# Norm factors of five groups spread by DRAM instead of by TensorE, and a new order in a run of small matmuls

## The chip, the core and the metric

The kernel runs on one core of a Trainium2 chip. The metric is the device time of one execution in microseconds (us); a time is the median of several runs. The engines are named as in the profile: PE is TensorE's matmuls, PEld its weight loads, DVE is VectorE, ACT is ScalarE, POOL is GpSimd, SP is SyncE, whose queue issues most of the loads. Each engine works through its own list of instructions in order. DRAM is the chip's main memory, SBUF and PSUM are the two memories beside the engines.

## What is computed

One decoder layer on 256 tokens of width 1024. One wide projection feeds a state-space scan (32 heads in 8 groups) and a causal attention (16 heads, two for each group), gates merge the two, an output projection and a gated feed-forward part follow. The part that the change touches is the end of the scan, where each group of 256 channels is normed by itself:

```python
y = y * jax.nn.silu(z.astype(jnp.float32))
yg = y.reshape(b, s, SSD_N_GROUPS, SSD_D_INNER // SSD_N_GROUPS)
yg = yg * lax.rsqrt(jnp.mean(yg * yg, axis=-1, keepdims=True) + RMS_EPS)
y = yg.reshape(b, s, SSD_D_INNER) * norm_w.astype(jnp.float32)
```

So each group has one factor for each of the 256 tokens (the rsqrt), and all 256 channels of the group are multiplied by it and by their own norm weight.

## The kernel before

Activations lie with channels on the 128 partitions and tokens along the row; a group's 256 channels are two halves of 128 x 256. Weights come in units of 1 MB by SP's queue into three buffers (`raw`). Each unit is split in two halves, and each half into a high part by ACT (`hi`, L96) and a low part by DVE (`lo`, L104); there are four buffers for each, which is two units. PE multiplies high by high, high by low and low by high (L165 to L167, L196 to L198, L460 to L462, and later L175 and L179).

The input stage (18 to 317 us of the profiled execution) is a loop over the groups g = 0 to 7. A group has the units `u_bc`, `u_x`, `u_qk`, `u_z`, and a value unit `u_v` or two gate units; between them lie two runs of small matmuls:

- `small_1(g)`, after `u_x(g)`: the scan's output of group g-1 (`s_y`, tile py, L521), the attention scores of g-1 (`a_s`, tile s_ps, L550), the attention output of g-2 (`a_o`, tile po, L608), the norm factors of g-2 (`s_pb`, tile pb, L242).
- `small_2(g)`, after `u_z(g)` or in the middle of the gate units: products for the scan of g (`s_cb`, `s_mx`, `s_xt`), the sum of squares of g-1 (`s_st`, tile stat, L231), and ACT's part of turning the probabilities of g-1 (`a_t`, L588).

How the norm goes: `s_y` leaves the gated output in yg and its squares in the buffer of zt, under the name sqy (L527, L528). `s_st` lets PE sum the squares over the partitions, which leaves the tokens on the partitions, 128 x 2; DVE makes the rsqrt by three Newton steps in small instructions (`rms_rstd`, the last is L222) and leaves it in ry, 128 x 2. `s_pb`, one group later, brings the factors back along the row on every partition: two PE matmuls (`rms_bcast`, L242) write them to pb in PSUM, and DVE multiplies yg by the norm weight and by pb (L537, two instructions). `split_pair` then makes the high part (ACT, L204) and the low part (DVE, L205) of yn, which only the projection behind the loop reads (from 303 us on). yg and zt have two buffers each, so those of group g come free for group g+2.

Attention: `a_s` lets DVE take the maxima (L557), ACT the exponentials and the scaling (L561, L565), POOL copy the probabilities as 16-bit halves (L571, two copies a group), and SP issue two transposing DMAs (L573), which stand in the same queue as the weight loads. `u_qk` copies q and k to SBUF (ACT, L435), POOL issues two small DMAs that swap their rotated rows (L437, L438), DVE multiplies by the cosines (L441), and `turn_qk` adds the sine part (L448, L449). POOL also issues the load of the scan's sums spread over the partitions (acsB, L424) and, in even groups, two loads of gate biases (L728).

What sets the order: PE's list is the program order. The lists of DVE, ACT, POOL and SP are made by a planner that follows the dependences, the program order as priority, and marks such as `tc.issue_after(x)` (not ahead of x in the list of that engine). A tile waits for the last reader of the buffer that it takes.

Of the kernel before, what the change touches and what calls it, by code (L numbers as in the profile page):

```python
# [8 lines left out]
F32 = mybir.dt.float32  # L9
# [4 lines left out]
ALU = mybir.AluOpType  # L14
# [5 lines left out]
P = 128  # L20
# [3 lines left out]
NG = 8  # L24
# [7 lines left out]
C_NW, C_D = 24, 40  # L32
# [5 lines left out]
C_ID = 256  # L38

WARM = 9  # L40


def block_kernel(tc, xtok_d, head_d, par_d, nf_d, con_d, rope_d, win_d, wgate_d, bg_d, watt_d, wssd_d, wout_d, wup_d, wdn_d, out_d):
    nc = tc.nc
    st = ExitStack()
    pool = lambda name, bufs=1, **kw: st.enter_context(tc.tile_pool(name=name, bufs=bufs, **kw))
    with st:
# [3 lines left out]
        dram = pool("dram", space=DRAM)  # L51
# [29 lines left out]
        def col(c):  # L81
            return par[:, c : c + 1]
# [141 lines left out]
        def rms_stat(sqs, inv_n):  # L224

            ps = ps_s.tile([P, 2, T], F32, tag="acc", bufs=1, name="stat")
            jobs = [(sq, ones[:, 0:1]) for sq in sqs]
            with tc.manual_schedule(engines=PE_ONLY):
                for i, (sq, one) in enumerate(jobs):
                    for c in range(2):  # L230
                        nc.tensor.matmul(ps[:, 0, c : c + 1], sq[:, c * P : c * P + P], one,  # L231
                                         start=(i == 0 and c == 0), stop=(i == len(jobs) - 1 and c == 1))
            y = work.tile([P, 2], F32, tag="ry", bufs=2, name="ry")
            with tc.high_priority():
                rms_rstd(y, ps[:, 0, 0:2], inv_n)
            return y

        def rms_bcast(y):

            pb = ps_s.tile([P, 2, T], F32, tag="ss", bufs=2, name="pb")  # L240
            for c in range(2):
                nc.tensor.matmul(pb[:, 0, c * P : c * P + P], y[:, c : c + 1].to_broadcast([P, P]), ident,  # L242
                                 start=True, stop=True)
            return pb[:, 0, :]
# [181 lines left out]
        def u_qk(g):  # L426
            hv = next_unit()
            if g == 0:

                with tc.issue_after(split_half.lo.ins):  # L430
                    conv_silu(S[0]["xs"], S[0]["x_ps"], (0, 1))
            ps = mm_tile()
            mm_unit(ps, hv, hn)
            raw = atp.tile([P, 2, T], F32, tag="qkraw", bufs=1, name="qkraw")
            S[g]["qk_copy"] = nc.scalar.activation(raw, ps, AF.Copy)  # L435
            sw = swaps[g % 2]
            nc.gpsimd.dma_start(sw[48:80:2], raw[49:80:2])  # L437
            nc.gpsimd.dma_start(sw[49:80:2], raw[48:80:2])  # L438
            qk = S[g]["qk"] = atp.tile([P, 2, T], F32, tag="qk", bufs=2, name="qk")
            cosb = rope[:, 0:1, :].to_broadcast([P, 2, T])  # L440
            nc.vector.tensor_tensor(qk, raw, cosb, op=ALU.mult)  # L441

        def turn_qk(g):

# [83 lines left out]
            nc.vector.tensor_tensor(sqy[:, 0], sqy[:, 0], sqy[:, 1], op=ALU.add)  # L528

        def s_st(g):  # L530
            S[g]["ry"] = rms_stat([S[g]["sqy"][:, 0]], 1.0 / 256)

        def s_pb(g):
            rb = rms_bcast(S[g]["ry"])
            yg = S[g]["yg"]
            for m in range(2):
                nc.vector.scalar_tensor_tensor(yg[:, m], yg[:, m], col(C_NW + 2 * g + m), rb, op0=ALU.mult, op1=ALU.mult)  # L537
                p = new_pair("yn")
                split_pair(p, yg[:, m])
                yn[2 * g + m] = p  # L540
# [154 lines left out]
        def small_1(g):  # L695
            if 0 <= g - 1 < NG:
                s_y(g - 1)
                a_s(g - 1)
            if 0 <= g - 2:
                a_o(g - 2)  # L700
                if g < NG:
                    s_pb(g - 2)

        def small_2(g):
            if g < NG:
# [10 lines left out]
        for g in range(NG):  # L716
            if g:
                u_bc(g)
                if g == 1:
                    s_mx(0, split_half.last_hi)  # L720
                u_x(g)
                small_1(g)
                load_acs(g)
            u_qk(g)
            if g % 2 == 0:
                cols = slice(256 * g, 256 * g + 512)
                for c in range(2):
                    tc.keep_in_program_order(nc.gpsimd.dma_start(gates[:, c, cols], bg_d[cols].partition_broadcast(P)))  # L728
            if g == 0:
                u_z(g, dt_sums)  # L730
                dt_turn()
                turn_qk(g)
                gate = u_gate(0)
                next(gate)
                load_acs(0)
                next(gate)
                next(gate)
                small_2(g)
                next(gate)
            elif g == NG - 1:  # L740
                u_z(g)
                turn_qk(g)
                small_2(g)
                u_v(g)
            elif g % 2:
                if g > 1:
                    u_v(g)
                    turn_qk(g)
                u_z(g)
                if g == 1:  # L750
                    turn_qk(g)
                small_2(g)
            else:
                u_z(g)
                turn_qk(g)
                gate = u_gate(g // 2)
                next(gate)
                next(gate)
                small_2(g)
                next(gate)  # L760
                next(gate)
# [319 lines left out]
```

## Time and profile before

| | |
|---|---|
| Time, median of 3 runs | 590.02 us (589.52 to 590.57) |
| The profiled execution, its own time | 589.48 us |
| Its span, from the first to the last instruction | 587.7 us |
| Granted TensorE clock, mean | 0.997 |
| PE busy | 579.0 us, 99% of the span |
| DVE busy | 464.0 us, 79% |
| ACT busy | 384.2 us, 65% |
| POOL busy | 33.7 us, 6% |
| Mean DMA rate | 191 GB/s |

The share of busy time says little for PE, since matmuls overlap and their ends are modelled: the start times tell what a matmul costs. What counts for the others is whether PE ever waits for them. The profile was taken of one execution; it is 0.54 us below the median of the runs.

### The profile page before, as it was taken

Reading aid. Unit: us, or ns where it says so; the run is one execution under the profiler, and the core shown is the slowest. Engines: PE = TensorE matmul, PEld = TensorE weight load, DVE = VectorE, ACT = ScalarE, POOL = GpSimd, SP = SyncE. Lnnn points to the kernel's source line nnn. Section 1 sums busy time; section 2 is a strip of 40 time slices with the busy share of each in tenths; the row PEclk is TensorE's granted clock in tenths of the full one; section 3 lists DMA queues with packets and bytes.
Section 4 is the critical chain, followed back from the end, with each engine's and each line's share of the span. In section 5 each row is a group of like instructions: output and inputs, shape, how many; then the busy total and the mean of one; then the engine's idle time right before and its main releaser. Section 6 shows DMA issues by size and latency. Waiting matters only on the chain.

```text
span 587.7 us, 9931 instructions
## 1 busy us (share of the span) xinstructions
PE 579.0 (99%) x3784; PEld 519.8 (88%) x3784; DVE 464.0 (79%) x891; ACT 384.2 (65%) x673; POOL 33.7 (6%) x55
## 2 busy tenths in 40 slices
PE   8999999999999999999999999999999999999995
PEld 8999999899998999989988888889888888888884
DVE  3996989899798997998996555768888898884643
ACT  2855697967769677695794434466777767774432
POOL 0010020301002010020100000000000000000100
PEclk9999999999999999999999999999999999999998
DMA  8766644874729737297436756554456545464601
GB/s 307 267 216 221 251 134 150 248 285 108 241 79 250 285 100 253 74 282 252 111 136 235 244 202 198 170 204 146 172 187 215 197 166 210 151 219 143 235 41 73
DMA packets 29136, 112.50 MB, mean 191 GB/s; under 512 B 13456, under 2 KB 13712, under 8 KB 17440
## 3 DMA queue, kind: packets, MB, share of 16 engines
q1 hardware_dynamic: 26320, 103.17, 52.1%
q0 software_dynamic: 2336, 6.85, 4.1%
q10 hardware_dynamic: 432, 1.84, 0.8%
q8 instruction: 30, 0.49, 0.3%
q14 instruction: 18, 0.15, 0.1%
HBM read 107.49 MB, written 1.08 MB: 185 GB/s over the span
## 4 chain that ended last, share of the span: by engine, by line
PE 98%; DMA 1%; DVE 0%; issue 0%; ACT 0%; DVEq 0%; ACTq 0%
PE up L175 12%; PE mm L165 11%; PE mm L167 11%; PE mm L196 11%; PE mm L166 11%; PE mm L198 11%; PE mm L197 11%; PE up L179 7%; PE py L521 2%; PE mm L294 1%; PE s_ps L550 1%; PE po L608 1%; PE mm L460 1%; PE mm L462 1%; PE mm L461 1%; PE pb L242 1%
## 5 line engine op out<-in xcount | busy, mean ns | idle before, releaser
L104 DVE TENSOR_TENSOR lo<-raw,hi 128x1024 fp32r<-128x1024 f32 x183 | 226.0, 1243 | 64.7 <-ACT hi L96 63.2
L96 ACT ACTIVATE hi<-raw 128x1024 fp32r<-128x1024 f32 x183 | 191.4, 1056 | 116.0 <-PE mm L198 62.0
L165 PE MATMUL mm<-hn,hi 128*128 128x256 f32 x504 | 143.6, 285 | 0.0
L167 PE MATMUL mm<-hn,lo 128*128 128x256 f32 x504 | 142.6, 283 | 0.0
L166 PE MATMUL mm<-hn,hi 128*128 128x256 f32 x504 | 142.6, 283 | 0.0
L165 PEld LDWEIGHTS mm<-hn,hi 128*128 128x128 f32 x504 | 96.6, 192 | 0.5 <-ACT hi L96 0.3
L166 PEld LDWEIGHTS mm<-hn,hi 128*128 128x128 f32 x504 | 96.7, 192 | 0.2
L167 PEld LDWEIGHTS mm<-hn,lo 128*128 128x128 f32 x504 | 96.6, 192 | 0.2 <-DVE lo L104 0.2
L175 PE MATMUL up<-xw,hi 128*128 128x512 f32 x320 | 76.3, 391 | 0.0
L175 PEld LDWEIGHTS up<-xw,hi 128*128 128x128 f32 x320 | 58.8, 188 | 11.4
L393 DVE SCALAR_TENSOR_TENSOR cacc<-mm,par,cacc 128x255 f32<-128x255 f32 (+2 forms) x96 | 44.1, 475 | 2.8 <-ACT cacc L389 2.3
L179 PEld LDWEIGHTS up<-xw,lo 128*128 128x128 f32 x320 | 41.0, 191 | 1.6
L179 PE MATMUL up<-xw,lo 128*128 128x256 f32 x320 | 41.5, 283 | 0.0
L197 PE MATMUL mm<-lo,act 128*128 128x512 f32 (+1 forms) x92 | 35.0, 380 | 0.0
L196 PE MATMUL mm<-hi,act 128*128 128x512 f32 (+1 forms) x92 | 34.9, 380 | 0.0
L198 PE MATMUL mm<-hi,act 128*128 128x512 f32 (+1 forms) x92 | 34.9, 380 | 0.0
L898 DVE SCALAR_TENSOR_TENSOR facc<-ab,par,facc 128x255 f32<-128x255 f32 (+1 forms) x44 | 21.2, 483 | 11.4 <-ACT facc L896 10.6
L196 PE MATMUL mm<-hi,hn 128*128 128x512 f32 x64 | 25.5, 398 | 0.0
L196 PE MATMUL mm<-hi,yn 128*128 128x512 f32 x64 | 25.2, 394 | 0.0
L198 PE MATMUL mm<-hi,hn 128*128 128x512 f32 x64 | 25.0, 391 | 0.0
L197 PE MATMUL mm<-lo,hn 128*128 128x512 f32 x64 | 25.0, 390 | 0.0
L198 PE MATMUL mm<-hi,yn 128*128 128x512 f32 x64 | 24.9, 390 | 0.0
(210 smaller groups left out, 978.8 us busy)
## 6 DMA issues: line engine op xcount, KB each, us to landing
raw<-in_win_dram SPq DMA_DIRECT2D x34, 1024.0 KB, 5.3
raw<-in_wup_dram SPq DMA_DIRECT2D x22, 1024.0 KB, 4.7
raw<-in_wdn_dram SPq DMA_DIRECT2D x10, 1024.0 KB, 4.9
raw<-in_wgate_dram SPq DMA_DIRECT2D x8, 1024.0 KB, 5.4
raw<-in_wssd_dram SPq DMA_DIRECT2D x8, 1024.0 KB, 4.9
acsB<-acsT_d POOLq DMA_DIRECT2D x8, 512.0 KB, 6.0
raw<-in_watt_dram SPq DMA_DIRECT2D x4, 1024.0 KB, 5.2
raw<-in_wout_dram SPq DMA_DIRECT2D x4, 1024.0 KB, 5.2
```

The source lines that it names most:

```text
L96: split_half.hi = nc.scalar.activation(hi[:, :n], raw[:, k0 : k0 + n], AF.Copy)
L104: split_half.lo = nc.vector.tensor_tensor(lo[:, :n], raw[:, k0 : k0 + n], hi[:, :n].bitcast(F32), op=ALU.subtract)
L165: nc.tensor.matmul(ps[m], wh, xh, start=a, stop=False)
L166: nc.tensor.matmul(ps[m], wh, xl, start=False, stop=False)
L167: nc.tensor.matmul(ps[m], wl, xh, start=False, stop=z)
L175: nc.tensor.matmul(ps[:, m].rearrange("p a b -> p (a b)"), hi[:, kk, m * P : m * P + P], act[k].rearrange("p a b -> p (a b)"), start=(k == ...
L179: nc.tensor.matmul(ps[:, m, 1], lo[:, kk, m * P : m * P + P], act[k][:, 0, :], start=False, stop=(k == len(tiles) - 1))
L196: nc.tensor.matmul(o, xh, wh, start=(k == 0 if apart else k0 + k == 0), stop=False)
L197: nc.tensor.matmul(o, xh, wl, start=False, stop=False)
L198: nc.tensor.matmul(o, xl, wh, start=False, stop=(k0 + k == nk - 1))
L393: nc.vector.scalar_tensor_tensor(acc[:, s:], src[:, m, : T - s], w(m, 3 - s), acc[:, s:], op0=ALU.mult, op1=ALU.add)
L898: nc.vector.scalar_tensor_tensor(acc[:, s:], src[:, : T - s], w(2 - s), acc[:, s:], op0=ALU.mult, op1=ALU.add)
```

## The change

For the groups 1 to 5 the factors no longer go through PE. Behind the rsqrt, `s_st` has POOL write ry to a small tensor in DRAM (each partition writes its two values, a piece of 8 bytes, 128 pieces), and then read it back for all 128 partitions (1 KB each) into the second half of sqy, which nobody needs any more. The second DMA waits until the first has landed. There the tokens lie interleaved (token t of both token halves side by side), so DVE reads every second value. `s_pb` of these groups has no matmul; its two multiplications read the factors from SBUF and are held behind the cosine product of two groups later, and `s_pb` itself moves from `small_1(g+2)` to behind `u_qk(g+2)`. The groups 0, 6 and 7 keep the matmuls. In every `small_1` the attention output (`a_o`) now comes ahead of the scores (`a_s`): scan, attention output, scores.

```diff
+BY_DRAM = (1, 6)
...
-            nc.vector.tensor_tensor(qk, raw, cosb, op=ALU.mult)
+            S[g]["qk_cos"] = nc.vector.tensor_tensor(qk, raw, cosb, op=ALU.mult)
...
         def s_st(g):
-            S[g]["ry"] = rms_stat([S[g]["sqy"][:, 0]], 1.0 / 256)
+            sqy = S[g]["sqy"]
+            ry = S[g]["ry"] = rms_stat([sqy[:, 0]], 1.0 / 256)
+            if BY_DRAM[0] <= g < BY_DRAM[1]:
+                rd = dram.tile([P, 2], F32, tag="rd", bufs=2, name="rd")
+                nc.gpsimd.dma_start(rd, ry)
+                S[g]["rb"] = sqy[:, 1].rearrange("p (t c) -> p c t", c=2)
+                nc.gpsimd.dma_start(sqy[:, 1], rd.rearrange("p c -> (p c)").partition_broadcast(P))
 
         def s_pb(g):
-            rb = rms_bcast(S[g]["ry"])
+            by_dram = "rb" in S[g]
+            rb = S[g]["rb"] if by_dram else rms_bcast(S[g]["ry"])
             yg = S[g]["yg"]
             for m in range(2):
-                nc.vector.scalar_tensor_tensor(yg[:, m], yg[:, m], col(C_NW + 2 * g + m), rb, op0=ALU.mult, op1=ALU.mult)
+                y = yg[:, m].rearrange("p (c t) -> p c t", c=2) if by_dram else yg[:, m]
+                with tc.issue_after(S[g + 2]["qk_cos"].ins) if by_dram else ExitStack():
+                    nc.vector.scalar_tensor_tensor(y, y, col(C_NW + 2 * g + m), rb, op0=ALU.mult, op1=ALU.mult)
                 p = new_pair("yn")
                 split_pair(p, yg[:, m])
                 yn[2 * g + m] = p
...
         def small_1(g):
             if 0 <= g - 1 < NG:
                 s_y(g - 1)
-                a_s(g - 1)
             if 0 <= g - 2:
                 a_o(g - 2)
-                if g < NG:
-                    s_pb(g - 2)
+            if 0 <= g - 1 < NG:
+                a_s(g - 1)
+            if 0 <= g - 2 and g < NG and "rb" not in S[g - 2]:
+                s_pb(g - 2)
...
             u_qk(g)
+            if g >= 2 and "rb" in S[g - 2]:
+                s_pb(g - 2)
```

## Rows read from the trace of the kernel before

**Rows 1.** The page: busy us, share of the span and instructions of each engine.
```profile
PE 579.0 (99%) x3784; PEld 519.8 (88%) x3784; DVE 464.0 (79%) x891; ACT 384.2 (65%) x673; POOL 33.7 (6%) x55
```

**Rows 2.** Waits of PE in the whole span: total us, times, longest.
```profile
PE warm L79 <- DVE eps L287: 1.1, 1, 1.1
PE mm L294 <- DVE xw L306: 0.4, 1, 0.4
```

**Rows 3.** Timeline of PE, the first run of group 5: start, us, operation.
```profile
204.12 1.52 PE L521 MATMUL py<-mx,xt 128*64 128x256 f32 x16
205.57 0.93 PE L550 MATMUL s_ps<-qk 64*128 64x128 f32 x8
206.42 0.87 PE L608 MATMUL po<-pt,vt 128*64 128x256 f32 x8
207.22 0.71 PE L242 MATMUL pb<-con,ry 128*128 128x128 f32 x4
...
207.89 0.28 PE L166 MATMUL mm<-hn,hi 128*128 128x256 f32 x1
```

**Rows 4.** Timeline of PE, the first run of group 1, without po and pb.
```profile
65.67 0.93 PE L550 MATMUL s_ps<-qk 64*128 64x128 f32 x8
...
66.75 0.28 PE L166 MATMUL mm<-hn,hi 128*128 128x256 f32 x1
```

**Rows 5.** Timeline of PEld, the same run of group 5: weight loads, idle before.
```profile
205.57 0.52 PEld L550 LDWEIGHTS s_ps<-qk 64*128 64x128 f32 x8 [0.17 <-issue]
206.42 0.63 PEld L608 LDWEIGHTS po<-pt,vt 128*64 128x64 f32 x8 [0.33 <-issue]
207.22 0.52 PEld L242 LDWEIGHTS pb<-con,ry 128*128 128x128 f32 x4 [0.17 <-DVE cacc L393]
```

**Rows 6.** Timeline of PE: py's last pair of matmuls ahead of s_ps.
```profile
205.36 0.28 PE L521 MATMUL py<-mx,xt 128*64 128x128 f32 x2
```

**Rows 7.** Stretch from group 4 to 5: us, PE, PEld, DVE, ACT, POOL, PEclk, DMA.
```profile
168.41:207.69 39.28, 39.28 (x291) 36.03 (x290) 35.06 (x72) 29.35 (x56) 4.51 (x7) 1.00 0.68 208
```

**Rows 8.** The tile lo: DVE's durations, and who waited for it.
```profile
L104 DVE TENSOR_TENSOR lo<-raw,hi x183: 1205/1219/1846, 18.2 to 570.5; 128x1024 fp32r<-128x1024 f32 x183
...
  PEld mm L167: 0.2, 1
```

**Rows 9.** Timeline of PE in group 2, where it waited for lo.
```profile
103.67 0.28 PE L166 MATMUL mm<-hn,hi 128*128 128x256 f32 x1
103.92 0.39 PE L167 MATMUL mm<-hn,lo 128*128 128x256 f32 x1
```

**Rows 10.** Timeline of DVE in group 4: scaling, two low parts, cosine product, next low part.
```profile
174.48 0.85 DVE L537 SCALAR_TENSOR_TENSOR yg<-yg,par,pb 128x256 f32<-128x256 f32 x2
175.25 2.98 DVE L104 TENSOR_TENSOR lo<-raw,hi 128x1024 fp32r<-128x1024 f32 x2
...
178.89 0.68 DVE L441 TENSOR_TENSOR qk<-qkraw,rope 128x512 f32<-128x512 f32 x1
179.49 1.84 DVE L104 TENSOR_TENSOR lo<-raw,hi 128x1024 fp32r<-128x1024 f32 x1
...
186.35 0.69 DVE L448 TENSOR_TENSOR swap<-swap,rope 128x512 f32<-128x512 f32 x1 [2.16 <-DMA swap<-qkraw]
```

**Rows 11.** Timeline of PE in group 4: first use of the second low part of rows 10.
```profile
180.24 0.40 PE L197 MATMUL mm<-lo,hn 128*128 128x512 f32 x1
```

**Rows 12.** Timeline of POOL in group 4: second copy of the probabilities.
```profile
179.27 0.99 POOL L571 COPY pt<-pr 128x768 uint16<-128x768 uint16 x1 [0.43 <-ACT pr L565]
```

**Rows 13.** POOL's DMA issues to DRAM (KB, us to landing) and from it (acsB).
```profile
acsT_d<-acsT POOLq DMA_DIRECT2D x1, 32.0 KB, 4.3
...
DMA to landing us min/median/max: 4.8/6.0/9.8
```

**Rows 14.** Timeline of DVE: last Newton step of ry, and the cosine product one group later.
```profile
124.04 0.16 DVE L222 SCALAR_TENSOR_TENSOR ry<-ra,ry 128x2 f32<-128x2 f32 x1
...
143.70 0.97 DVE L441 TENSOR_TENSOR qk<-qkraw,rope 128x512 f32<-128x512 f32 x1 [0.26 <-ACT qkraw L435]
```

## The prediction

> **What bounds the kernel now.** I read the page first: PE is busy for 579.0 us of the 587.7 us span, DVE for 464.0 and ACT for 384.2 [rows 1]. Since the ends of matmuls are modelled, that alone doesn't prove that PE is the bound. The list of PE's waits does: in the whole span there are two, 1.1 and 0.4 us long, both before the first weights are used [rows 2]. I then looked for hidden waits, starts of successive matmuls that lie further apart than usual. For the tile lo, which DVE makes for PE, there is one wait in the span, 0.2 us [rows 8]; it sits in group 2, where two starts lie 0.25 us apart [rows 9], against 0.10 to 0.12 us between such matmuls where PE is fed (11 units in 1.24 us, below). So PE goes from one matmul to the next without a break, and each 0.1 us that leaves PE's list shortens the kernel by 0.1 us, as long as DVE, ACT and the loads stay ahead of a PE that comes a little earlier.
>
> How far ahead they are is read in a tight place, the even groups, where DVE is busy for 35.06 of 39.28 us [rows 7]. In group 4 DVE makes two low parts by 175.25 + 2.98 = 178.23 [rows 10], and PE first uses the second at 180.24 [rows 11]: 2.0 us to spare. In group 2 the reserve is gone [rows 9].
>
> **What leaves PE.** The run after `u_x` in group 5 shows py at 204.12, s_ps at 205.57, po at 206.42, pb at 207.22 and the second matmul of the next unit at 207.89 [rows 3]: 1.45 + 0.85 + 0.80 + 0.67 = 3.77 us. I take that second matmul as the end, because the first one behind a run starts early and delays its neighbour. In group 1 there is no pb, and from s_ps to that same second matmul it is 66.75 - 65.67 = 1.08 us [rows 4].
>
> Then the order. py and po load weights of one shape (128*64), s_ps of another (64*128), and pb and the units of a third (128*128). At each change of shape the weight load stands idle, 0.17 us ahead of s_ps, 0.33 ahead of po and 0.17 ahead of pb [rows 5]: it can't run under the matmul before it. The new order puts po right behind py, so one change goes. Its worth: py's last pair of matmuls starts at 205.36 [rows 6] and s_ps at 205.57, 0.21 us for a pair of 128 columns. The other pairs of py (four of 256 columns and three of 128, or 11 units of 128 columns) take 1.45 - 0.21 = 1.24 us, 0.11 a unit. So 0.10 us of the 0.21 are the change of shape, and py ahead of po costs 1.35 instead of 1.45. po ahead of s_ps still has a change behind it, as it has ahead of pb: 0.80.
>
> - New run without pb: 1.35 + 0.80 + 1.08 = 3.23 us, 0.54 less. If the change of shape costs as much as before, py keeps its 1.45: 3.33, 0.44 less. If po's first pair is no longer slowed either (by the spare 0.05 us or so that py's first pair also shows in its 1.24 us over 11 units), 0.59 less. I take 0.56, between the last two, since the idle of 0.33 us ahead of po in [rows 5] is the largest of the three. There are five such runs, in the groups 3 to 7: 2.8 us (2.2 to 2.95).
> - Two more runs have po ahead of s_ps but keep pb or never had it, the one in group 2 and the one behind the loop: 0.10 to 0.15 us each. In group 2 PE already waits for lo [rows 9], so I count nothing there; behind the loop 0.13.
>
> Sum: 2.8 + 0.13 = 2.93 us.
>
> **What the change adds, and what hides it.** Ten DMA issues on POOL, which is busy for 33.7 us in all [rows 1]. The first of each pair waits for ry, the second for the first to land. Queued behind it on POOL are the next run's copies of the probabilities, the swap DMAs and, where it comes later, the load of acsB. The trace has no write of 8-byte pieces. The nearest row is acsT_d, a write of 32 KB to DRAM, 4.3 us to landing, and the nearest read is acsB, spread over the partitions, 4.8 to 9.8 us [rows 13]. So the round trip lies between 9 and, taking the worst read twice, 20 us; I take 4.3 + 6.0 = 10.3, because one row is a write to DRAM and the other a spread read. The reader comes late: ry is done at 124.20 and the cosine product that the scaling follows ends at 143.70 + 0.97 = 144.67 [rows 14], 20.5 us later. So the wait is hidden. The Trainium skill, "DMA: Bandwidth & Descriptors", section "Anatomy of one DMA — SWDGE (gpsimd) path", gives a POOL DMA a fixed cost of about 2 us, most of it the receipt of the write and long with DRAM as the target; by it the round trip would be an estimated 4 us, the cover larger still, and the chance of the late landing below smaller. The row of 4.3 us for one write speaks against the lower figure.
>
> DVE's work stays the same in number: two multiplications, 0.85 us in all [rows 10], and two low parts of yn, now behind the cosine product instead of ahead of the two low parts of weights. Those come up to 0.85 us earlier, which more than pays for the 0.56 us by which PE comes sooner. Behind the cosine product DVE has the idle time that ends at 186.35, 2.16 us [rows 10], in which the moved work fits. A step of two values along the row has no row here; between the cost of the same elements in PSUM (nothing added) and a doubled 0.85 us, I take nothing, since DVE's idle time would hide it.
>
> ACT's copies of yn move with it, and ACT's tanh of the next z now waits for the scaling, as it takes that buffer; queued behind the tanh are the scan's exponentials and the next high parts. PE's scores come 0.8 us later against py, so the maxima, exponentials, POOL's copies and SP's transposing DMAs, which stand in one queue with the weight loads, may be up to 0.8 - 0.1 us later; DVE was still at other work in the tight groups, so I count nothing.
>
> **The forecast.** 590.02 - 2.93 = 587.1 us. The profiled execution, 589.48 us (a span of 587.7 and 1.8 around it), would be 586.55; I go from the median, 0.54 above it. With the low and high ends of the run's terms 586.5 to 587.9.
>
> **Rivals.** First, the cover in the even groups gives out. There the scaling comes when POOL copies probabilities (179.27 to 180.26 in group 4 [rows 12]), and the low part beside that copy took 1.84 us against a median of 1.22 [rows 8, 10]. The Trainium skill, "SBUF — State Buffer", section "SBUF: two separate sides", has the rule: a DVE operation with two inputs in SBUF and a GpSimd operation that reads SBUF exclude one another for the whole instruction. The low part reads two tiles in SBUF, and so will the new scaling, where the old one read pb from PSUM: it can be caught as that low part was. If it then stands ahead of a low part, that one is late by 0.85 + 0.68 (the two low parts of yn, together as many elements as the cosine product of 0.68 us [rows 10]) + up to 0.99 = 2.5 us, against 2.0 us to spare less 0.56: PE waits 1.1 us in the two groups 4 and 6, and gives back 2.2. Time: 589.3 at worst, 588.2 if half of it happens. For it: the reserve is small. Against: the total of DVE's work before that use is what it was.
>
> Second, the removed wait on PE is replaced everywhere: the planner's new order of DVE and ACT costs about as much as each run saves (0.56), because high parts come later behind the tanh. Time: 589.9. Against it: outside the even groups nothing in the trace shows PE waiting.
>
> Third, slower. The second DMA waits on POOL behind the next run's copies instead of ahead of them, if the planner puts it there. Then it is issued at 180.3 in group 4 [rows 12] and lands 4.8 to 9.8 us later [rows 13], at 185 to 190; DVE, whose scaling stands in order, is held from 179.57 on [rows 10] for 5.5 to 10.5 us, less 2.0 to spare. In the groups 4 and 6 that is 7 to 17 us: 594 to 604. It decides from the point at which the round trip exceeds 20.5 us [rows 14]. Against it: program order has both DMAs a group ahead of those copies.
>
> That the change doesn't do what it says would be the low end of the sum, the change of shape not saved: 587.7.
>
> **How the numbers follow.** Within 0.2% (1.2 us, 588.8 to 591.2) a measurement can hardly tell this kernel from the one before. The forecast with its ends has 0.64, the first rival 0.18, two thirds of it still below 588.8, the second 0.09, the third 0.09. So faster 0.64 + 0.12 = 0.76, the same 0.06 + 0.09 = 0.15, slower 0.09. The range takes in the forecast, a wobble of 0.5 us of the median below its low end, and the first rival: 586.0 to 589.3.
>
> **What would show it.** Right: twenty matmuls of L242's kind fewer, a run of group 5 that takes about 3.2 us, weight loads without idle time ahead of po, PE without new waits, the scaling on DVE without idle time before it. Wrong: idle time of DVE that ends with a DMA into zt, low parts of weights of 1.8 us or more at new places, or starts of PE further apart in the groups 2, 4 and 6.

## The result and the profile after

| | before | after |
|---|---|---|
| Time, median (14 executions each) | 590.1 us (589.5 to 594.5) | 595.9 us (591.2 to 599.2) |
| Ratio to before, 95% interval | | 1.0082 [1.0053, 1.0111] |
| The profiled execution, its own time | 589.5 us | 592.2 us |
| Its span | 587.7 us | 590.4 us |

The changed kernel is slower by 0.8%, where 0.5% faster was forecast. Its profiled execution is among its fastest. The executions of the kernel before lie in two clusters about 4 us apart, those of the changed kernel are spread over 8 us; one early load, the first acsB, lands late in some of them, and experiments below take that out. Ratios are taken over the executions within 1.5% of the fastest of their kernel, which leaves out four of the ten of the new order alone, and none elsewhere.

PE has less to do, as forecast (compare [rows 1]), and POOL 10.7 us more:

```profile
PE 577.7 (98%) x3764; PEld 518.4 (88%) x3764; DVE 463.8 (79%) x891; ACT 382.7 (65%) x673; POOL 44.4 (8%) x65
```

The run of group 5 on PE in the changed kernel (start, us, operation), which answers to [rows 3]:

```profile
206.03 1.52 PE L523 MATMUL py<-mx,xt 128*64 128x256 f32 x16
207.38 0.82 PE L621 MATMUL po<-pt,vt 128*64 128x256 f32 x8
208.13 0.93 PE L563 MATMUL s_ps<-qk 64*128 64x128 f32 x8
208.99 0.38 PE L167 MATMUL mm<-hn,hi 128*128 128x256 f32 x1
209.21 0.28 PE L168 MATMUL mm<-hn,hi 128*128 128x256 f32 x1
```

From py to the second matmul of the next unit it is 209.21 - 206.03 = 3.18 us, against 3.77 before: 0.59 us less, and the same in the other four runs that lost pb. So the gain is there. The waits of PE in the whole span show where it went (total us, times, longest; left out are the two of [rows 2], here 1.1 and 0.2 us):

```profile
PE po L621 <- ACT vt L467: 1.3, 1, 1.3
PE mm L169 <- DVE lo L106: 1.2, 2, 0.8
...
PE mm L167 <- ACT hi L98: 0.8, 1, 0.8
PE pt_ps L607 <- ACT pr L578: 0.7, 1, 0.7
```

Two of the places lie in group 4, where the timeline of PE has these starts:

```profile
192.12 0.39 PE L200 MATMUL mm<-hi,hn 128*128 128x512 f32 x1
193.31 0.39 PE L167 MATMUL mm<-hn,hi 128*128 128x256 f32 x1 [0.80 <-ACT hi L98]
193.53 0.28 PE L168 MATMUL mm<-hn,hi 128*128 128x256 f32 x1
194.57 0.39 PE L169 MATMUL mm<-hn,lo 128*128 128x256 f32 x1 [0.75 <-DVE lo L106]
```

The matmuls stand 1.19 and 1.04 us apart instead of 0.23 and 0.12, which is 0.96 and 0.92 us lost, and 0.1 on the one behind. Two lie in the run behind the loop:

```profile
300.11 1.52 PE L523 MATMUL py<-mx,xt 128*64 128x256 f32 x16
302.93 0.87 PE L621 MATMUL po<-pt,vt 128*64 128x256 f32 x8 [1.30 <-ACT vt L467]
...
310.55 0.52 PE L607 MATMUL pt_ps<-con,pr 128*128 128x128 f32 x3
311.79 0.83 PE L607 MATMUL pt_ps<-con,pr 128*128 128x128 f32 x3 [0.72 <-ACT pr L578]
312.46 0.61 PE L244 MATMUL pb<-con,ry 128*128 128x128 f32 x4
```

From py to po it is 2.82 us against 1.35 in the other runs, 1.47 lost; from pt_ps to pb it is 1.91 us against 0.69 before (309.06 to 309.75), 1.22 lost. The wait for lo in group 2 [rows 9] is 0.5 us longer (0.76 us from start to start), and the whole kernel is 0.66 us late by the time of the first group, before any of the changed steps: the weight load that starts at 41.37 us before starts at 42.03. These 0.66 us arise among the first matmuls and differ by execution: in two other executions of the changed kernel they are 0.12 and 0.15. Sum: 5 x 0.59 and 2 x 0.10 for the order in the two other runs is a gain of 3.15; the losses are 1.98 + 1.47 + 1.22 + 0.51 + 0.66 = 5.84. The difference, 2.69 us, is that of the two spans, 2.7.

Why hi is late in group 4 is seen on ACT, which goes through its list in order. Changed kernel, then kernel before, from the copies of the transposed probabilities (pt<-pr) to the next high parts:

```profile
189.93 1.08 ACT L601 ACTIVATE pt<-pr 128x768 uint16<-128x768 uint16 x1 [3.64 <-DMA pr<-pt]
191.28 1.08 ACT L601 ACTIVATE pt<-pr 128x768 uint16<-128x768 uint16 x1 [0.27 <-DMA pr<-pt]
192.23 3.88 ACT L98 ACTIVATE hi<-raw 128x1024 fp32r<-128x1024 f32 x4
```

```profile
186.11 1.08 ACT L588 ACTIVATE pt<-pr 128x768 uint16<-128x768 uint16 x1
187.44 1.08 ACT L588 ACTIVATE pt<-pr 128x768 uint16<-128x768 uint16 x1 [0.25 <-DMA pr<-pt]
188.39 1.98 ACT L96 ACTIVATE hi<-raw 128x1024 fp32r<-128x1024 f32 x2
```

Before, the transposing DMAs landed as ACT came to them. Now ACT stands 3.64 us, and the high parts behind, whose data landed at 185.15, start at 192.23. The low part is late for the same reason, since DVE makes it from the high part:

```profile
193.29 1.23 DVE L106 TENSOR_TENSOR lo<-raw,hi 128x1024 fp32r<-128x1024 f32 x1 [1.01 <-ACT hi L98]
```

In the whole span ACT waits 6.7 us for these DMAs, against 0.2 before. The landing of the two DMAs in that stretch (min/median/max us from the issue), changed kernel and before:

```profile
DMA to landing us min/median/max: 9.5/10.1/10.7
```

```profile
DMA to landing us min/median/max: 7.1/7.9/8.7
```

The longer landing isn't peculiar to the new order: with the factors by DRAM and the old order (first experiment below) the two took 11.3 and 10.0 us. What the order does move is their issue. The first one is issued 13.9 us behind the start of py in the changed kernel, 12.5 before, and 11.7 with the old order and DRAM. Of this the scores make 0.65 us (they start 2.10 us behind py instead of 1.45). ACT's list adds to it: a high part that waits for PE now stands ahead of the first exponentials, which before came as soon as their maxima were there. Changed kernel, then kernel before:

```profile
174.15 1.06 ACT L98 ACTIVATE hi<-raw 128x1024 fp32r<-128x1024 f32 x1 [1.31 <-PE mm L168]
175.12 0.39 ACT L574 ACTIVATE pr<-pr,sm 128x128 f32<-128x128 f32 x1
```

```profile
173.38 0.40 ACT L561 ACTIVATE pr<-pr,sm 128x128 f32<-128x128 f32 x1 [0.57 <-DVE sm L559]
```

The round trip of the factors, on the other hand, harms nobody: DVE never waits for it. Issue to landing in the changed kernel, median of five each:

```profile
zt<-rd POOLq DMA_DIRECT2D x5, 128.0 KB, 5.6
...
rd<-ry POOLq DMA_DIRECT2D x5, 1.0 KB, 6.8
```

### The profile page after: what moved, and what is told of

Same layout as the page of the kernel before. It is cut to its first block, busy times and chain, and to the rows that moved or that the text cites. A ratio compares the mean times of both kernels' runs of the same rounds, so it can differ in the third digit from the quotient of the medians.

```text
span 590.4 us, 9902 instructions
## 1 busy us (share of the span) xinstructions
PE 577.7 (98%) x3764; PEld 518.4 (88%) x3764; DVE 463.8 (79%) x891; ACT 382.7 (65%) x673; POOL 44.4 (8%) x65
## 4 chain that ended last, share of the span: by engine, by line
PE 79%; DVE 7%; ACT 6%; DMA 5%; issue 2%; POOL 0%; SPq 0%; ACTq 0%; DVEq 0%
PE up L177 12%; PE mm L198 10%; PE mm L200 10%; PE mm L199 10%; PE mm L167 8%; PE mm L169 7%; PE mm L168 7%; PE up L181 6%; DVE lo L106 2%; ACT hi L98 2%; DVE cacc L395 2%; PE mm L296 1%; DMA swap<-qkraw 1%; DMA acsB<-acsT_d 1%; PE py L523 1%
## 5 line engine op out<-in xcount | busy, mean ns | idle before, releaser
L914 DVE SCALAR_TENSOR_TENSOR facc<-ab,par,facc 128x255 f32<-128x255 f32 (+1 forms) x44 | 21.2, 483 | 11.3 <-ACT facc L912 10.6
L398 ACT ACTIVATE th<-cacc 128x256 f32<-128x256 f32 x32 | 13.2, 414 | 18.7 <-DVE cacc L395 18.7
L198 PE MATMUL mm<-hi,yn 128*128 128x512 f32 x64 | 25.2, 394 | 0.0
```

The lines of the kernel that those rows point to most:

```text
L198: nc.tensor.matmul(o, xh, wh, start=(k == 0 if apart else k0 + k == 0), stop=False)
L914: nc.vector.scalar_tensor_tensor(acc[:, s:], src[:, : T - s], w(2 - s), acc[:, s:], op0=ALU.mult, op1=ALU.add)
```

## The experiments

**Theory:** the new order costs more than it gives, since scores that come later make the transposing DMAs later, and ACT stands behind these in order, ahead of high parts and of the copy of vt. **Rivals:** the round trip or the moved scaling costs; the loss is spread over all groups; POOL and DVE collide at the memory that they share; the rest is chance in a load.

**Which part of the change costs?** The first kernel has the factors by DRAM and the old order:

```diff
         def small_1(g):
             if 0 <= g - 1 < NG:
                 s_y(g - 1)
+                a_s(g - 1)
             if 0 <= g - 2:
                 a_o(g - 2)
-            if 0 <= g - 1 < NG:
-                a_s(g - 1)
```

> The factors of groups 1 to 5 go by DRAM as in the changed kernel, but every run keeps the old order: scan, scores, attention output. If the new order is what costs (it puts the attention output right behind the value unit whose copy it reads, and the scores, and with them the transposing DMAs that ACT waits for in order, later), this kernel loses nothing and saves the five pairs of pb: 5 x 0.44 = 2.2 us, 587.9 us against 590.1, with executions within 1.5 us of one another as before. If the DRAM round trip or the moved scaling costs, it stays at 592 or above and spreads as the changed kernel does (591 to 599).

Measured: median 589.9 us beside 594.24 for the kernel before on the same chip, ratio 0.9953 [0.9921, 0.9985]. So DRAM alone gains. How much is less sure: 4 of its 10 executions are above 593 us, against 24 of the 31 beside it, which is the first acsB; the fastest of each are 588.34 and 589.98. The second has the new order alone, with the factors on PE in all groups:

```diff
-BY_DRAM = (1, 6)
+BY_DRAM = (1, 1)
```

> Only the new order; all factors are spread by TensorE's matmuls as before. If the new order costs, the last run shows the attention output waiting for the copy of the values (1.47 us) and the turning of the probabilities waiting (1.06 us), the groups 2 and 4 show waits for high and low parts, and the time is 592 to 596 us with a spread. If DRAM costs, only the last run's 2.5 us less 7 x 0.15 us are left: 591.5 us, with executions within 1.5 us of one another.

Measured: median 598.85 us, 591.0 to 604.0, ratio 1.0012 [0.9968, 1.0055], too scattered to say more than that nothing is gained. In its profile (599.9 us) PE waits 1.53 and 0.92 us in group 4 and 1.0 us for pt_ps without any DMA to or from rd; it doesn't wait ahead of po. The profile of DRAM alone shows no wait there either, so by these two profiles it takes both parts of the change to make vt late. The changed kernel beside them, unaltered:

> The changed kernel once more, on the same chip as the three others, for a second profiled execution: 591 to 599 us. If the late transposing DMAs make the spread, an execution with another time shows the difference in the waits of ACT for these DMAs in the groups 2, 4 and 6 and in PE's waits behind them, and nowhere else by more than 0.3 us.

Measured: 596.4 us, ratio 1.0043 [1.0018, 1.0069]; the kernel before beside it has its median at 594.24. The waits stand at the same places: hi and lo in group 4 (1.21 and 0.92 us), po (1.76), pt_ps. But the expectation, that the executions differ by these waits alone, missed: of the 6.0 us by which this one is longer than the first profile, 4.2 come in group 2, where PE waits 3.2 us for lo and is slower behind the wait. ACT had waited 7.2 us for the first acsB.

**Where does it cost?** The old order in the run behind the loop alone:

```diff
+            if g == NG:
+                a_s(g - 1)
             if 0 <= g - 2:
                 a_o(g - 2)
-            if 0 <= g - 1 < NG:
+            if 0 <= g - 1 < NG and g < NG:
                 a_s(g - 1)
```

> The changed kernel with the old order in the run behind the loop alone, so that the scores stand between the value unit and the attention output again. Both theories: the two waits there (1.47 and 1.06 us) go and the 0.15 us of that run with them, so 2.4 us less than the changed kernel in the same job, and the spread of its executions stays.

Measured: 594.7 us, 1.7 below the changed kernel beside it (596.4), where 2.4 was expected, ratio 1.0021 [0.9986, 1.0056]. The wait for pt_ps is gone, the one for vt shrinks to 1.0, though both were to go. Then the new order in the odd groups alone (`g % 2` in place of `g < NG`, and even groups in the place of `g == NG`):

> The changed kernel with the new order in the runs of odd groups alone (1, 3, 5, 7); the runs of groups 2, 4, 6 and the last one have the old order. Theory: the loss sits where DVE and ACT have no reserve, the even groups and the last run, so this kernel loses the 1.9 us of group 4, the 1.3 to 1.6 ahead of po and the 1.06 ahead of pt_ps, and is at 588 to 590 us, up to 0.3 us better than the one with the old order everywhere. Rival (the new order costs in every run, as the scores of any group come 0.75 us later): half of the loss stays, about 1 us of waits in the odd groups 5 and 7, 591 to 592.

Measured: median 591.57, ratio 1.0002 [0.9967, 1.0037]; the fastest four executions are at 588.9 to 589.5, where the theory put them, the other six at 591.1 to 597.2. PE's waits in its profile (589.5 us) are 0.3 us for lo in group 4 and 0.7 for vt. So, by the waits, most of the loss sits in the even groups and behind the loop. The odd groups aren't free: vt is late although the run behind the loop has the old order, because ACT stands 1.5 us for the second transposing DMA of group 7.

**Is it ACT's place behind the DMAs?** Here the two copies are taken from ACT and given to POOL:

```diff
-                with tc.issue_after(S[g + 1]["z_tanh"].ins):
-                    for pr, pt in zip(S[g]["pr"], S[g]["pt"]):
-                        nc.scalar.activation(halves(pt), apart(pr), AF.Copy)
+                for pr, pt in zip(S[g]["pr"], S[g]["pt"]):
+                    nc.gpsimd.tensor_copy(halves(pt), apart(pr))
```

In the changed kernel:

> The changed kernel with the two copies that put the transposed probabilities together (pt<-pr, behind the transposing DMAs) moved from ACT to POOL. Theory: the new order's loss comes from ACT, which stands in order behind these DMAs; then the waits of PE in group 4 (0.96 + 0.92 us for hi and lo, at 192 to 194 us) and ahead of po in the last run (1.3 to 1.6 us) go, 3.2 us in all, while the 1.06 us ahead of pt_ps stays, since its chain s_ps, maxima, exponentials, transposes holds no such copy: about 3 us less than the changed kernel in the same hour, or 590 to 593 us against 593.4 to 599.8 so far on this chip. Rival (DVE is slowed by the later POOL copies through the memory they share, and that makes lo late): the waits in group 4 stay or grow, since POOL now copies four times a group, and the time is that of the changed kernel or more, 596 to 600.

In the kernel before, as the control:

> The kernel before with the same move of these copies to POOL, and nothing else: the control. Theory: in the kernel before ACT waits 0.2 us in all for a transposing DMA and PE waits for none of it, so the move brings nothing, 0 to 0.5 us. Rival: ACT's 1.05 us a copy, 15 us in all, is what makes high parts late in any order; then this kernel is faster by 1 us or more too. If POOL's copies slow DVE down, it is slower by 1 us or more, and that amount is to be taken off the reading of the other kernel with copies on POOL.

Measured: the changed kernel comes to 591.9 us, ratio 1.0011 [0.9988, 1.0035]; the control to 592.25 (1.0009 [0.9981, 1.0036]), its fastest execution at 591.1 against 589.6 for the kernel before beside it. PE's waits in the changed kernel with copies on POOL:

```profile
PE pt_ps L606 <- ACT pr L578: 1.6, 1, 1.6
PE mm L169 <- DVE lo L106: 1.3, 1, 1.3
...
PE mm L198 <- ACT qkraw L437: 0.8, 1, 0.8
```

The waits in group 4 and ahead of po are gone; those listed lie in group 2 and at pt_ps. POOL's copies have a price of their own, some 1.5 us by the fastest executions of the control. The same move with the factors by DRAM and the old order:

> Norm factors by DRAM, the runs in the old order (scan, scores, attention), the copies on POOL: put together from the two parts that should each help or cost nothing. Theory: the time of the same kernel with the copies on ACT (588.3 to 590.2, and 593.2 to 593.8 in executions in which the first acsB lands late) or up to 0.8 us less, as its one own wait in group 4 (0.80 us for lo) goes. Rival (copies on POOL slow DVE): 1 us or more above it.

Measured: 592.05 us, ratio 1.0000 [0.9969, 1.0031], fastest at 589.55 against 588.34 with the copies on ACT: the rival's case. So POOL is the wrong place for them. The cleaner test leaves them on ACT, two high parts later, in the even groups:

```diff
                 s_st(g - 1)
-                a_t(g - 1)
+                if g % 2 or g == NG:
+                    a_t(g - 1)
...
                 small_2(g)
                 next(gate)
                 next(gate)
+                a_t(g - 1)
```

> The changed kernel, with the two copies pt<-pr of the groups 2, 4 and 6 still on ACT but two high parts later in its order; nothing on POOL changes. Theory (ACT stands in order behind the transposing DMAs): PE's two waits in group 4 (0.96 and 0.92 us) go, the waits ahead of po (1.3 to 1.6) and pt_ps (1.06) in the last run stay, as group 7 is left alone: 1.9 us less than the changed kernel of the same call. Rival (DVE and POOL collide at the memory they share, and the low parts are late for that): at most the first of the two waits goes, which is for a high part; less than 1 us. The wait in group 2 for lo (0.64 us, or 3 us where the first acsB lands late) is not touched by either.

and, beside it, the changed kernel unaltered:

> The changed kernel unaltered, beside the other three. All theories: 592 to 599 us, with a scatter three times that of the kernel before, PE's waits in group 4, ahead of po and ahead of pt_ps as in its other profiles.

Measured: 592.7 us (ratio 1.0030 [0.9997, 1.0064]) against 595.9 (1.0065 [1.0029, 1.0102]). PE's waits with the late copies:

```profile
PE po L621 <- ACT vt L467: 1.8, 1, 1.8
PE mm L169 <- DVE lo L106: 1.1, 2, 0.6
...
PE pt_ps L607 <- ACT pr L578: 0.7, 1, 0.7
```

The wait for hi is gone, those behind the loop stay, as expected. Of the two waits in group 4 one remains, 0.73 us from start to start, for a low part. So 1.2 of the 1.9 us go with ACT's standing. In the changed kernel both waits came of it; with it gone, DVE's own list sets the next limit. DVE stands 3.69 us for the swap DMA of q and k, until 186.10, and then works without a pause up to this low part, which takes its usual 1.22 us with no copy on POOL beside it. So what remains isn't the rival's collision. Unaltered, the changed kernel showed here no wait in group 4 at all: its two transposing DMAs landed 8.7 and 7.6 us after their issue, not 10.7 and 9.5, and ACT stood 1.7 us. How long they take differs from execution to execution, and the wait with it. All three causes at once, late copies and the old order behind the loop:

> The same copies late, the new order in the loop's runs, the old order in the run behind the loop: all three causes named for the loss of the changed kernel are taken away, and what was forecast of PE's list stays. Theory: 2.8 us under the kernel before, less 0.6 in group 2, or 587.2 to 588.5 us in executions in which the first acsB lands early. Rival (the new order has further costs, spread over all groups, that the three do not cover): 590 or more, not better than the kernel before.

Measured: median 591.5, ratio 1.0003 [0.9971, 1.0036], fastest 588.68. No execution reaches the theory's range; three are within 0.7 us above it. PE still waits 0.5 us ahead of po and 0.7 for lo in group 2.

**What makes the rest of the median?** ACT's wait for the first acsB, at 50 us: the changed kernel's profiled execution, and another of the changed kernel (595.8 us):

```profile
ACT mx L496 <- DMA acsB<-acsT_d: 2.7, 1, 2.7
```

```profile
ACT mx L496 <- DMA acsB<-acsT_d: 5.9, 1, 5.9
```

The queues in the two, SP's weight loads and POOL's two DMAs (start, us, issue):

```profile
42.03 7.62 SPq L93 DMA_DIRECT2D raw<-in_win_dram  x3
42.70 0.52 POOL L672 DMA_DIRECT2D acsT_d<-acsT  x1 [3.31 <-ACT acsT L671]
47.50 0.56 POOL L426 DMA_DIRECT2D acsB<-acsT_d  x1 [4.28 <-DMA acsT_d<-acsT]
```

```profile
41.49 7.62 SPq L93 DMA_DIRECT2D raw<-in_win_dram  x3
42.17 0.52 POOL L672 DMA_DIRECT2D acsT_d<-acsT  x1 [3.32 <-ACT acsT L671]
47.64 0.55 POOL L426 DMA_DIRECT2D acsB<-acsT_d  x1 [4.95 <-DMA acsT_d<-acsT]
```

In the second the write of acsT_d lands 0.67 us later after its issue, and the load of acsB, issued that much later against SP's next weight loads, takes 8.5 us instead of 5.9. DVE and ACT are then 3 us late, and in group 2, which has no reserve [rows 9], PE waits 3.1 us for lo. The next edit has SP issue that one load, where it stands ahead of the weight load:

```diff
-            nc.gpsimd.dma_start(acsB, acsT_d[4 * g : 4 * g + 4, :].partition_broadcast(P))
+            (nc.gpsimd if g else nc.sync).dma_start(acsB, acsT_d[4 * g : 4 * g + 4, :].partition_broadcast(P))
```

In the kernel before:

> The kernel before with the load of the first acsB issued by SP, ahead of the weight load that otherwise starts 0.4 to 1.5 us before it, instead of by POOL. If the late landing of this load (ACT waits 5 to 7 us for it at 50 us instead of 2.7 to 3.2) makes the upper cluster of times at 593.5 to 596, that cluster is gone: nearly all runs at 589.5 to 591. If not, about a quarter or more of the runs stay at 593.5 to 596.

In the changed kernel:

> The same edit in the changed kernel. Theory A (the rest of its median over its fastest executions is the first acsB, which lands late more often in it): the runs draw together at 591 to 593, median about 592. Theory B (waits on transposing DMAs that differ by execution): the scatter stays, 591 to 597, with a median of 594 to 595, and only the runs above 597 go.

Measured: the kernel before 589.5 us, all executions from 589.1 to 590.4, ACT's wait 0.9 us; unedited beside it, 13 of 35 are above 593. The changed kernel 592.07, from 589.7 to 594.4. So with acsB in time the loss is 592.07 - 589.52 = 2.55 us, 0.43%, near the 2.7 us of the two profiled spans. The other 3.2 of the 5.8 us come with the first acsB: with the edit no execution is above 594.43, without it 10 of 14 are, against 1 of 14 of the kernel before. Theory A of the expectation held for the median and B for what scatter remains. That the load lands late more often in the changed kernel is read from the times, and why isn't shown: none of the changed steps has run by then, and on another chip 24 of 31 executions of the kernel before were above 593 too. The scatter that remains is seen in the edited kernel's profiled execution (593.7 us), ACT and then PE behind the loop:

```profile
299.65 1.06 ACT L601 ACTIVATE pt<-pr 128x768 uint16<-128x768 uint16 x1 [3.02 <-DMA pr<-pt]
...
302.46 0.57 ACT L467 ACTIVATE vt<-mm 128x512 f32<-128x512 f32 x1
```

```profile
298.61 1.52 PE L523 MATMUL py<-mx,xt 128*64 128x256 f32 x16
303.18 1.55 PE L621 MATMUL po<-pt,vt 128*64 128x256 f32 x8 [3.05 <-ACT vt L467]
```

It is the same pattern in group 7: ACT stands 3.02 us for a transposing DMA, the copy of vt is late by as much, and PE by 3.05 us. This DMA is the second of the two, and a weight load is now issued between them: it took 7.4 us to land, the first 2.8. In the kernel before both were issued ahead of that load and took 2.8 and 3.2. So the changed kernel was run with all of it taken away: acsB by SP, late copies in the even groups, and those of group 7 alone on POOL:

```diff
+                if g == NG - 2:
+                    for pr, pt in zip(S[g]["pr"], S[g]["pt"]):
+                        nc.gpsimd.tensor_copy(halves(pt), apart(pr))
+                    return
```

> The changed kernel, new order everywhere, with the first acsB by SP, the copies pt<-pr of groups 2, 4 and 6 two high parts later on ACT, and those of group 7 on POOL, so that ACT doesn't stand behind a transposing DMA ahead of the copy of vt. Theory: the wait ahead of po (1.5 to 3.2 us) and those of group 4 go, the scatter shrinks to that of the kernel before with acsB by SP (1.3 us), what stays is the 0.8 us ahead of pt_ps: 588 to 589.5 us. Rival (the wait ahead of po comes from ACT being loaded in group 7 as such, by the moved copies of yn): it stays at 1 us or more, 590 to 593.

Measured: 590.3 us, from 589.4 to 592.1, ratio 0.9960 [0.9938, 0.9983]. The wait ahead of po is gone and the scatter falls from 4.7 to 2.7 us; but pt_ps waits 1.6 us and PE 1.3 for lo in group 4, so it ends above the range that was expected. The whole cost of the order isn't this one wait.

**What is the best that comes of it?** The old order with the factors by DRAM, first with the late copies:

> Norm factors by DRAM, all runs in the old order, copies pt<-pr of the even groups two high parts later. Theory: the gain of the five pb's, 5 times some 0.5 us, with nothing given back in group 4 (0.80 us there with the copies in their old place): about 587.5 to 588.5 us in executions in which the first acsB lands early, 2 to 2.5 under the kernel before. Rival (the round trip by DRAM itself costs, through the transfers it adds on POOL's queue and the later scaling): it stays at 588.5 to 590, as with the copies in their old place.

Measured: median 589.9, ratio 0.9987 [0.9960, 1.0015], early executions at 588.3 to 590.6, where the kernel with the copies in their old place also is. Nothing was gained by the late copies here. With acsB by SP:

> Norm factors by DRAM, old order in all runs, copies of the even groups two high parts later, first acsB by SP. Theory: the lower cluster of the same kernel without the last edit, 588.3 to 589.2, for all runs; against the kernel before with its own first acsB by SP about 1.3 us less, against the kernel before as it is up to 0.4% less. Rival: SP, held up by the wait for acsT_d, starts the next weight load some 0.5 us later and PE waits for it; then 590 or more.

Measured: 588.15 us, from 587.0 to 589.1, ratio 0.9930 [0.9908, 0.9953], the best of all kernels, 1.37 us under the kernel before with the same acsB (589.52). What PE still waits for in it is this:

```profile
PE mm L169 <- DVE lo L106: 0.9, 1, 0.9
PE mm L199 <- DVE lo L106: 0.5, 1, 0.5
```

Both lie in group 4, and again behind the swap DMA, which took 9.0 us here and 6.1 in the kernel before:

```profile
184.86 0.69 DVE L450 TENSOR_TENSOR swap<-swap,rope 128x512 f32<-128x512 f32 x1 [4.72 <-DMA swap<-qkraw]
185.47 1.22 DVE L106 TENSOR_TENSOR lo<-raw,hi 128x1024 fp32r<-128x1024 f32 x1
```

Before, DVE made three low parts of weights between the cosine product and this product with swap, and stood 2.16 us [rows 10]; now the moved scaling and the low parts of yn are there too, only two low parts of weights come ahead of it, and the next one stands behind it in the list. With the new order in the loop's runs:

> The new order in the loop's runs with all repairs: copies of the even groups two high parts later, old order behind the loop, first acsB by SP. If the order itself is worth 0.1 us a run on PE and costs nothing else, 0.3 to 0.7 us less than the kernel with the old order and the same edits; if the later scores still cost through group 2 (0.6 to 0.9 us for lo there) or the other even groups, equal or up to 1 us more, with more scatter.

Measured: 589.4 us, from 588.0 to 591.7, ratio 0.9963 [0.9936, 0.9991]: 1.3 above the old order, with more scatter, and outside what was expected either way. In its profile (591.2 us) PE waits 0.7 us for lo in group 4, and ahead of po although the scores stand there again:

```profile
PE po L621 <- ACT vt L467: 2.3, 1, 2.3
```

ACT had stood 3.1 us for the second transposing DMA of group 7, whose own run has the new order. And the old order with group 7's copies on POOL:

> Norm factors by DRAM, old order everywhere, first acsB by SP, copies of the even groups later, and those of group 7 on POOL too. The old order has scores ahead of po, so that the copy of vt has 0.85 us more; theory: 0 to 0.5 us less than without the last edit (587.0 to 589.1, median 588.15) and less scatter. Rival: the POOL copies hold up DVE ahead of py in the last run, as in the kernel with all copies on POOL (0.68 us): 0.3 to 0.8 us more.

Measured: 588.95 us, ratio 0.9926 [0.9898, 0.9953], from 588.2 to 590.3, with 0.7 us of waiting ahead of py for DVE: the rival's case. The changed kernel with the same edits (590.3, above) ran beside it: 1.35 us more for the new order, as in the pair before.

## Why the prediction was wrong

**PE as the bound, and the gain of a run.** Right. The forecast was 0.56 us a run, the trace has 0.59. From py to po it is 1.35 us as forecast, so one change of shape goes; po takes 0.75 where the sum has 0.80, the low end that the prediction named. Two slips change nothing in this: the ends of the forecast from 590.02 are 586.9 and 587.7, not 586.5 and 587.9, and the low parts of yn stood behind the two low parts of weights before, not ahead of them.

**The round trip by DRAM.** Right: 6.8 + 5.6 = 12.4 us, within the 9 to 20 given and hidden. The estimate from the page of the Trainium skill, "DMA: Bandwidth & Descriptors", section "Anatomy of one DMA — SWDGE (gpsimd) path", some 4 us in all, was low by a factor of three: a write of 1 KB alone took 6.8 us beside the weight loads.

**The step that failed: the scores.** The prediction saw that scores, maxima, POOL's copies and the transposing DMAs come up to 0.7 us later, and counted nothing, "DVE was still at other work in the tight groups". It looked at DVE, and the reserve that gave out was ACT's. ACT's copies behind the DMAs stand in its list ahead of high parts; before, ACT came to the first at 186.11 and it had just landed, so the reserve was nil. And the 0.7 us didn't stay 0.7: behind a high part in ACT's list the exponentials start at 175.12 instead of 173.38, and POOL's first copy at 178.27 instead of 176.19; the DMAs then take 10.1 us instead of 7.9, as long as they also do with DRAM and the old order. ACT's standing went through to PE because PE's cover was small there: before, the high part at 188.39 was done 3.1 us ahead of its first use at 192.52, and the low part at 190.83 0.7 us ahead of 192.75. The prediction had read its 2.0 us to spare 12 us earlier, at 180.24. In the changed kernel's profile this costs 1.98 us in group 4; moving ACT's copies wins back 1.2, and then DVE's list sets the limit.

**The step that was missing: the run behind the loop.** It was put down as a gain of 0.13 us. There po reads vt, the unit right ahead of the run, through a copy on ACT; in the old order s_ps stood between and covered that copy with 0.85 us, in the new one po follows py directly, and the copy itself is late behind the DMAs of group 7: 1.47 us, and 3.2 in another execution. Later scores also delay the probabilities that PE turns itself: 1.22 us. With the old order there the wait for pt_ps is gone. The one ahead of po isn't: it is 0.5 to 2.3 us in the four profiles with the old order there and the new one in the run of group 7. So the lost cover is only part of that wait; the other part is the failed step again, scores that come later in the run of group 7.

**The first rival** named one right place, group 4 (no profile shows PE waiting in group 6), and about the right price (1.1 us of waiting for lo there; 1.4 in the best kernel). Its collision shows too: the scaling with the factors in SBUF takes 0.48 us at the median and 1.05 at the longest, and POOL's copies, 0.97 us at the median before, now 1.30:

```profile
L550 DVE SCALAR_TENSOR_TENSOR yg<-yg,par,zt x10: 472/480/1046, 142.7 to 289.4; 128x256 f32<-128x256 f32 x10
```

But that isn't what PE waits for. In the best kernel DVE is through with the scaling and the low parts of yn at 180.1 and then stands 4.72 us for the swap DMA; the late low parts are those behind it in DVE's list. In this profile the place in the list and the longer landing of that DMA make the wait, and what the collision cost DVE is lost in its standing; no run moves those low parts to prove it. By the Trainium skill, "SBUF — State Buffer", section "SBUF: two separate sides", a DVE operation with two inputs in SBUF and a GpSimd operation that reads SBUF shut each other out; the 1.05 us beside a copy on POOL, against 0.47 for the next one without, agree with it. The second rival's price (the gain given back) was exceeded; the third didn't occur.

**The range** allowed 0.5 us for the scatter of the median. The trace of before couldn't show the late acsB, since it was taken of an execution in which the load came early, and the three times ahead of the prediction (589.52 to 590.57) had none of the later cluster; of the 14 beside the changed kernel two are in it.

## What to carry to other kernels

Ask for every engine of a chain that an edit makes later what stands behind the waiting instruction in that engine's list, and how long before that instruction its input landed; an input that lands just in time is a reserve of nil, though no wait shows. Where one edit both removes work and reorders, time the two apart: here the removal alone gains 0.1 to 0.5% in three comparisons, and the order costs 1.3 us in each of the two pairs of kernels that differ in nothing else. What neither part does alone they can do together, as with the wait ahead of po: look at the reserve that is left, not only at the waits. Where the times of a kernel lie in two clusters, look for the load whose landing differs, before reading anything else from the medians.

## What the runs showed of the hardware

A wait of PE of some 3 us cost more than itself. In the execution with the late acsB, PE did 0.88 us of work between 104 and 108 us, and its granted clock in the next 5 us was 0.50, the level of 1.2 GHz; in the profiled execution with the early acsB it stayed at 1.00 (stretch, us, PE, PEld, DVE, ACT, POOL, PEclk, DMA):

```profile
108.00:113.00 5.00, 5.00 (x24) 4.90 (x24) 5.00 (x6) 3.51 (x6) 4.05 (x6) 0.50 0.92 255
```

```profile
108.00:113.00 5.00, 5.00 (x24) 4.12 (x23) 3.07 (x3) 5.00 (x14) 1.98 (x2) 1.00 1.08 310
```

Matmuls that start 0.12 us apart in the second started 0.21 us apart in the first, and against that profile PE lost a further 2.65 us by 113.7. Behind the 3.05 us ahead of po the clock was 0.54 for 3.5 us. The waits of 0.8 to 1.5 us in the changed kernel's own profiled execution left it at 1.00.

One small DMA landed with the large one that was started ahead of it: the 32 KB of acsT_d, issued 0.67 us behind a weight load of 1 MB, landed 0.2 us behind it, 4.5 us after the issue and 5.2 in the other execution, in which the weight load took 5.7 us instead of 5.0. And 0.67 us in the issue of acsB, against weight loads that started on time, went with 2.5 us more from issue to landing.
